# Seven-product weight pairs in a two-layer decoder trunk: a fourth pair, sums formed in place, and half of the plain low parts formed by accumulating DMA

## The chip, the cores and the metric

The kernel runs on one core of a Trainium2 chip. The metric is the device time of one execution in microseconds (us). The kernel before takes 2154.96 us, the median of three runs that lie between 2154.92 and 2155.69 us. A profile records one execution; its span runs from the first to the last instruction, and the execution's own time is a little longer.

## What is computed

Two pre-norm residual layers work on 256 tokens of width 2048. Each layer has a mixer (layer 0: sliding-window attention beside a matrix memory; layer 1: attention with forget gates) and then a SwiGLU block. The change touches only the SwiGLU block and what prepares its input:

```python
def swiglu(xn, w_gate, w_up, w_down):
    return (jax.nn.silu(xn @ w_gate) * (xn @ w_up)) @ w_down
# x: (256, 2048); w_gate, w_up: (2048, 5632); w_down: (5632, 2048); all float32
```

## The kernel before, in words

**Precision.** TensorE multiplies float32r tiles, which keep fewer bits than float32. So each operand is split into a high part (a cast, `hi`) and a low part (`lo`, the raw value minus the high part), and each block product is three matmuls: high times high, high times low, low times high (`three`, L350 to L353). The result is a 128x512 block in a PSUM bank.

**Chunks and half chunks.** The 16 blocks of the k axis (2048 / 128) are taken in eight pairs. `load_raw` (L94) brings two k blocks of 512 columns of one weight matrix, 512 KB, by one DMA of the SP queue into a raw tile of 128x1024. `split_chunk` (L147) makes `hi` on ACT (L150, a cast) and `lo` on DVE (L151, a subtraction). There are six `hi` and six `lo` tiles (pool `wp`) and four raw tiles (pool `wr`).

**The gate and up products.** The 5632 hidden columns are 11 groups of 512. For each group, `pair_group` (L358) works on both matrices and both token tiles of 128, over the eight k pairs, in the order of the tuple `ORDER`: each entry says whether the pair is plain (0) or mixed (1), and which k pair it is.

- A *plain* pair has 2 matrices x 2 k blocks x 2 token tiles = 8 block products, 24 matmuls. Its two half chunks (one of gate, one of up) are split as above.
- A *mixed* pair treats the same 2x2 blocks of x and of the weights by a scheme with 7 block products, 21 matmuls. Four weight sums are formed by DVE from the raw blocks (L386 to L389) into a tile `t4`, and `t4` is then split into `ht` (ACT, L246) and `lt` (DVE, L247) in two halves of 128x1024; the gate half chunk is split by L150 and L151, and one block of up by L246 and L247 with 128x512. The four sums of x blocks (`sx`) are made once per layer, when the mixer's output projection ends (`sums_of`, L208 to L216, called from `split_scaled`). Four of the seven products go to banks of their own (`prods`) and are combined once per group (L412 to L416).

Before the change three of the eight pairs are mixed: 5 x 24 + 3 x 21 = 183 matmuls for each group. Mixed pairs load into two raw tiles of the pool `fp`; `t4` has one buffer, `ht` and `lt` have two each.

**After the products.** DVE adds the two kinds of banks (L438), ACT takes the silu (L440), DVE multiplies (L442), TensorE transposes (L450, eight small matmuls per group), and the result is split into `mh` and `ml` (L246, L247).

**Down.** Hidden groups are taken in three parts per layer (3, 4 and 4 groups, `PARTS`). After each part the down projection over its 12 or 16 k blocks follows, with the same `pair_group` and one or two mixed pairs (`DOWN`). With 11 groups and two layers there are 22 gate and up groups in all.

**What sets the order.** The instructions of each engine run in program order, and that order is not the one of the source: the kernel is built with `schedule_with_timeline_sim=True`, so a planner simulates the program and places each instruction on its engine's queue by its own times. In the trace the matmuls of neighbouring pairs are therefore mixed with each other. Loads are issued from the SP queue, which holds nothing else; a load waits there until the tile it fills has been released. The POOL queue holds very little while the SwiGLU blocks run.

**Memory.** `dynamic_dma_scratch_size=8192` (L908) reserves that many bytes of every partition for the descriptors of DMAs that POOL issues.

Of the kernel before, what the change touches and what calls it, by code (L numbers as in the profile page):

```python
# [7 lines left out]
F32 = mybir.dt.float32  # L8
F32R = mybir.dt.float32r
AF = mybir.ActivationFunctionType  # L10
ALU = mybir.AluOpType
# [4 lines left out]
P = 128  # L16
D = 2048
# [4 lines left out]
NB = 512  # L22
CK = 2
# [7 lines left out]
OFF_QM, OFF_KM, OFF_VM, OFF_OM = 1536, 2048, 2560, 3584  # L31
CAP = 15.0
FILL = 24
ORDER = ((0, 0), (0, 1), (1, 2), (0, 4), (1, 3), (0, 5), (1, 6), (0, 7))
DOWN = {
    6: ((0, 0), (0, 1), (1, 2), (0, 3), (0, 4), (0, 5)),
    8: ((0, 0), (0, 1), (1, 2), (0, 3), (0, 4), (1, 5), (0, 6), (0, 7)),
# [11 lines left out]
def trunk(  # L49
# [20 lines left out]
    nc = tc.nc  # L70
# [7 lines left out]
    wr = ctx.enter_context(tc.tile_pool(name="wr", bufs=4))  # L78
# [15 lines left out]
    def load_raw(w, k0, c0, n, pool=wr):  # L94
        raw = pool.tile([P, CK, NB], F32, tag="raw", name="raw")
        nc.sync.dma_start(
            raw[:, :, 0:n], w[k0 * P : (k0 + CK) * P, c0 : c0 + n].rearrange("(k p) n -> p k n", p=P)
        )
        return raw
# [5 lines left out]
    for n in range(4):  # L105
# [7 lines left out]
        out=ident, in_=ident, pattern=[[-1, P]], compare_op=ALU.not_equal, fill=1.0, base=0, channel_multiplier=1  # L113
# [5 lines left out]
        out=upper, in_=ones, pattern=[[1, P]], compare_op=ALU.is_ge, fill=0.0, base=0, channel_multiplier=-1  # L119
# [20 lines left out]
    gain_columns(0)  # L140


    def load_chunk(w, k0, c0, n):
        raw = ahead.pop(0) if ahead else load_raw(w, k0, c0, n)
        return split_chunk(raw, n)

    def split_chunk(raw, n):  # L147
        hi = wp.tile([P, CK, NB], F32R, tag="hi", name="hi")
        lo = wp.tile([P, CK, NB], F32R, tag="lo", name="lo")
        nc.scalar.copy(hi[:, :, 0:n], raw[:, :, 0:n])  # L150
        nc.vector.tensor_tensor(  # L151
            out=lo[:, :, 0:n], in0=raw[:, :, 0:n], in1=hi[:, :, 0:n].bitcast(F32), op=ALU.subtract
        )
        return hi, lo
# [34 lines left out]
    sums = {}  # L189
# [55 lines left out]
    def split_plain(dst_h, dst_l, src):  # L245
        nc.scalar.copy(dst_h, src)  # L246
        nc.vector.tensor_tensor(out=dst_l, in0=src, in1=dst_h.bitcast(F32), op=ALU.subtract)  # L247
# [110 lines left out]
    def pair_group(fp, par, lhs, sums, mats, order):  # L358
        plain = [[bank(par, "acc") for _ in range(NT)] for _ in range(2)]
        prods = None  # L360
        kinds = [kind for kind, _ in order]
        t0, t1 = slice(0, P), slice(P, 2 * P)
        for pos, (kind, pair) in enumerate(order):
            k0 = 2 * pair
            if not kind:
                last = pos == len(order) - 1
                walk = [(i, t) for i in range(CK) for t in range(NT)]
                if last:
                    walk.sort(key=lambda it: it[1])
                for m, (w, c0) in enumerate(mats):  # L370
                    hi, lo = load_chunk(w, k0, c0, NB)
                    for i, t in walk:
                        ah, al = lhs(k0 + i)
                        ts = slice(t * P, (t + 1) * P)
                        three(
                            plain[m][t], ah[:, ts], al[:, ts], hi[:, i, :], lo[:, i, :],
                            pos == 0 and i == 0, last and i == CK - 1,
                        )
                continue
            first, last = 1 not in kinds[:pos], 1 not in kinds[pos + 1 :]  # L380
            if first:
                prods = [bank(1 - par, "prod") for _ in range(4)]
            ra, rb = (load_raw(w, k0, c0, NB, fp) for w, c0 in mats)
            hg, lg = split_chunk(ra, NB)
            t4 = fp.tile([P, 4, NB], F32, tag="t4", name="t4", bufs=1)
            nc.vector.tensor_tensor(out=t4[:, 0, :], in0=rb[:, 0, :], in1=ra[:, 0, :], op=ALU.subtract)  # L386
            nc.vector.tensor_tensor(out=t4[:, 1, :], in0=rb[:, 1, :], in1=rb[:, 0, :], op=ALU.subtract)
            nc.vector.tensor_tensor(out=t4[:, 2, :], in0=rb[:, 1, :], in1=t4[:, 0, :], op=ALU.subtract)
            nc.vector.tensor_tensor(out=t4[:, 3, :], in0=ra[:, 1, :], in1=t4[:, 2, :], op=ALU.subtract)  # L389
            hu = wp.tile([P, CK, NB], F32R, tag="hi", name="hi")  # L390
            lu = wp.tile([P, CK, NB], F32R, tag="lo", name="lo")
            split_plain(hu[:, 1, :], lu[:, 1, :], rb[:, 1, :])
# [20 lines left out]
        nc.vector.tensor_tensor(out=u2, in0=prods[3], in1=c[:, 0, :], op=ALU.add)  # L413
        nc.vector.tensor_tensor(out=c[:, 1, :], in0=prods[2], in1=u2, op=ALU.add)
        nc.vector.tensor_tensor(out=c[:, 2, :], in0=prods[1], in1=u2, op=ALU.add)
        nc.vector.tensor_tensor(out=c[:, 3, :], in0=prods[1], in1=c[:, 1, :], op=ALU.add)  # L416
        return plain, c

    def ffn(layer, fp, sx, sd, key, idx_next=None, key_next=None, finish=None):
# [6 lines left out]
        for g0, g1 in zip(PARTS, PARTS[1:]):  # L426
            end = g1 == PARTS[-1]
            nk = 4 * (g1 - g0)
            order = DOWN[nk // 2]
            for g in range(g0, g1):  # L430
                par = (g1 - 1 - g) % 2
                plain, c = pair_group(
                    fp, par, x_of, sums_x, [(w_gate[layer], g * NB), (w_up[layer], g * NB)], ORDER
                )
                for m in range(2):
                    for t in range(NT):
# [8 lines left out]
                for half in range(2):  # L445
# [5 lines left out]
                    pair = 2 * (g - g0) + half  # L451
# [22 lines left out]
            gf = None  # L474
            wd = w_down[layer][4 * g0 * P : 4 * g1 * P, :]
            for n0 in (0, 2):
# [7 lines left out]
                    fp, 1 - n0 // 2, m_of, sums_d, [(wd, n0 * NB), (wd, (n0 + 1) * NB)], order  # L484
                )
                if end and idx_next is None:
                    gf = fp.tile([P, D], F32, tag="t4", name="gf", bufs=1)
                    nc.gpsimd.dma_start(gf, norm_final.partition_broadcast(P))
                for m in range(2):
                    for t in range(NT):  # L490
# [23 lines left out]
    with tc.tile_pool(name="ev", bufs=1) as ev:  # L514
# [138 lines left out]
        with tc.tile_pool(name="mp", bufs=1) as mp:  # L653
            dt_ = mp.tile([P, ML_H, NT, P], F32, name="dt_")
            for g in range(2):
                pb = pm.tile([P, 2, NT, P], F32, tag="pm", name="pb")
                for i in range(2):
# [7 lines left out]
                    op=ALU.add,  # L665
# [257 lines left out]
```

## Time and profile before

| What | Before |
|---|---|
| median of three runs | 2154.96 us |
| profiled execution, its own time | 2154.99 us |
| its span | 2153.3 us |
| TensorE matmul (PE) busy | 2137.1 us, 99% of the span |
| VectorE (DVE) busy | 1668.7 us, 77% |
| ScalarE (ACT) busy | 1164.1 us, 54% |
| GpSimd (POOL) busy | 37.7 us, 2% |
| DMA from the SP queue, share of the 16 DMA engines | 58.3% |
| granted TensorE clock, mean | 0.998 |

Busy time is the time in which an engine works on at least one instruction; neighbouring instructions overlap, so the distance from start to start is what one of them costs, not its own duration. A wait row says which engine waited, at which line, and for what. A window row gives the busy time of each engine inside one stretch of the span, and the share of the DMA engines. In group rows the shapes stand as partitions x elements.

### The profile page before, as it was taken

The page shows a single profiled execution, that of the slowest core. Times are in us where ns is not written, and L with a number is a line of the kernel's source. Part 1 is how long each engine was busy: PE and PEld are TensorE (multiplying, and loading weights), DVE is VectorE, ACT ScalarE, POOL GpSimd, SP SyncE. Part 2 cuts the span into 40 slices and gives each one's busy share as a digit, 9 for nine tenths or more (in the row PEclk, how much of TensorE's full clock was granted, in tenths as well). Part 3 has the DMA queues.
Part 4 walks back from the last instruction along what each step waited for, and adds up shares of the span by engine and source line. Part 5 has one row for each costly group of instructions (what it writes and reads, how often), then busy time and mean ns, then how long its engine had stood idle before and what let it go on. Part 6 is the DMA issues. An engine that isn't in the chain of part 4 may idle for free.

```text
span 2153.3 us, 27002 instructions
## 1 busy us (share of the span) xinstructions
PE 2137.1 (99%) x9932; PEld 1774.6 (82%) x9932; DVE 1668.7 (77%) x2136; ACT 1164.1 (54%) x1514; POOL 37.7 (2%) x61
## 2 busy tenths in 40 slices
PE   8999999999999999999999999999999999999998
PEld 7888888888888888888888888888888888888886
DVE  6665567898889988998755555668988898888984
ACT  6564455655555545655545444555655555555553
POOL 2010000000000000000010000000000000000000
PEclk9999999999999999999999999999999999999999
DMA  8444555656665666656575554656556566656563
GB/s 266 147 157 145 169 171 191 208 194 203 203 201 180 210 195 205 200 191 196 160 234 166 166 177 149 212 176 205 195 192 206 190 200 209 196 199 203 178 213 127
DMA packets 213541, 408.37 MB, mean 190 GB/s; under 512 B 12736, under 2 KB 21024, under 8 KB 213152
## 3 DMA queue, kind: packets, MB, share of 16 engines
q1 hardware_dynamic: 212736, 402.90, 58.3%
q0 software_dynamic: 624, 3.72, 0.5%
q8 instruction: 78, 1.28, 0.2%
q14 instruction: 55, 0.45, 0.1%
q10 hardware_dynamic: 48, 0.02, 0.0%
HBM read 404.48 MB, written 2.11 MB: 189 GB/s over the span
## 4 chain that ended last, share of the span: by engine, by line
PE 98%; ACT 1%; issue 0%; DMA 0%; DVE 0%; DVEq 0%; POOLq 0%; POOL 0%; ACTq 0%
PE acc L353 17%; PE acc L352 17%; PE acc L351 17%; PE acc L173 10%; PE acc L175 10%; PE acc L174 10%; PE prod L353 4%; PE prod L352 4%; PE prod L351 4%; PE pf L450 1%; PE pt L224 1%; PE p L275 1%; PE ptm L258 1%; PE po L326 1%; PE pp L318 0%
## 5 line engine op out<-in xcount | busy, mean ns | idle before, releaser
L150 ACT CAST hi<-raw 128x1024 fp32r<-128x1024 f32 (+1 forms) x692 | 707.5, 1033 | 648.5 <-PE acc L353 314.3
L151 DVE TENSOR_TENSOR lo<-raw,hi 128x1024 fp32r<-128x1024 f32 (+1 forms) x692 | 825.7, 1201 | 288.1 <-ACT hi L150 285.9
L352 PE MATMUL acc<-lo,xh 128*128 128x512 f32 x946 | 368.4, 389 | 0.0
L353 PE MATMUL acc<-hi,xl 128*128 128x512 f32 x946 | 367.5, 391 | 0.0
L351 PE MATMUL acc<-hi,xh 128*128 128x512 f32 x946 | 365.2, 389 | 0.0
L173 PE MATMUL acc<-hi,xh 128*128 128x512 f32 (+3 forms) x736 | 276.8, 377 | 0.7 <-ACT hi L150 0.7
L175 PE MATMUL acc<-hi,xl 128*128 128x512 f32 (+3 forms) x736 | 276.9, 377 | 0.0
L174 PE MATMUL acc<-lo,xh 128*128 128x512 f32 (+3 forms) x736 | 276.4, 375 | 0.0
L247 DVE TENSOR_TENSOR lt<-t,ht 128x1024 fp32r<-128x1024 f32 x168 | 200.1, 1219 | 28.8 <-ACT ht L246 27.8
L246 ACT CAST ht<-t 128x1024 fp32r<-128x1024 f32 x168 | 174.6, 1053 | 81.1 <-PE prod L353 44.3
L352 PEld LDWEIGHTS acc<-lo,xh 128*128 128x128 f32 x946 | 177.6, 188 | 37.0
L353 PEld LDWEIGHTS acc<-hi,xl 128*128 128x128 f32 x946 | 177.6, 188 | 36.3
L351 PEld LDWEIGHTS acc<-hi,xh 128*128 128x128 f32 x946 | 177.7, 188 | 36.1
L352 PE MATMUL acc<-lo,mh 128*128 128x512 f32 x514 | 200.4, 390 | 0.0
L353 PE MATMUL acc<-hi,ml 128*128 128x512 f32 x514 | 199.4, 389 | 0.0
L351 PE MATMUL acc<-hi,mh 128*128 128x512 f32 x514 | 198.9, 389 | 0.0
L173 PEld LDWEIGHTS acc<-hi,xh 128*128 128x128 f32 x736 | 139.0, 189 | 24.9 <-ACT hi L150 1.1
L175 PEld LDWEIGHTS acc<-hi,xl 128*128 128x128 f32 x736 | 139.1, 189 | 24.4 <-issue 0.8
L174 PEld LDWEIGHTS acc<-lo,xh 128*128 128x128 f32 x736 | 139.1, 189 | 24.0 <-issue 0.7
L173 PE MATMUL acc<-hi,mh 128*128 128x512 f32 x320 | 125.8, 393 | 1.2 <-ACT mh L246 1.2
L174 PE MATMUL acc<-lo,mh 128*128 128x512 f32 x320 | 125.7, 393 | 0.0
L175 PE MATMUL acc<-hi,ml 128*128 128x512 f32 x320 | 124.0, 390 | 0.0
(299 smaller groups left out, 2726.8 us busy)
## 6 DMA issues: line engine op xcount, KB each, us to landing
raw<-in_w_gate_dram SPq DMA_DIRECT2D x176, 512.0 KB, 3.8
raw<-in_w_up_dram SPq DMA_DIRECT2D x176, 512.0 KB, 4.4
raw<-in_w_down_dram SPq DMA_DIRECT2D x176, 512.0 KB, 4.3
raw<-in_w_in_odd_dram SPq DMA_DIRECT2D x88, 512.0 KB, 3.8
raw<-in_w_in_even_dram SPq DMA_DIRECT2D x64, 512.0 KB, 4.2
raw<-in_w_out_even_dram SPq DMA_DIRECT2D x32, 512.0 KB, 3.7
raw<-in_w_out_odd_dram SPq DMA_DIRECT2D x32, 512.0 KB, 4.0
raw<-in_w_in_odd_dram SPq DMA_DIRECT2D x8, 272.0 KB, 2.8
```

The costliest lines, as they stand in the source:

```text
L150: nc.scalar.copy(hi[:, :, 0:n], raw[:, :, 0:n])
L151: nc.vector.tensor_tensor(out=lo[:, :, 0:n], in0=raw[:, :, 0:n], in1=hi[:, :, 0:n].bitcast(F32), op=ALU.subtract)
L173: nc.tensor.matmul(o, ah[:, ts], hi, start=(k == 0), stop=False)
L174: nc.tensor.matmul(o, ah[:, ts], lo, start=False, stop=False)
L175: nc.tensor.matmul(o, al[:, ts], hi, start=False, stop=(k == k_all - 1))
L224: nc.tensor.transpose(pt[:, i, t, :], h[:, t, k * P : (k + 1) * P], ident)
L246: nc.scalar.copy(dst_h, src)
L247: nc.vector.tensor_tensor(out=dst_l, in0=src, in1=dst_h.bitcast(F32), op=ALU.subtract)
L258: nc.tensor.transpose(pt[:, i, :], s_, ident)
L351: nc.tensor.matmul(o, ah, hi, start=start, stop=False)
L352: nc.tensor.matmul(o, ah, lo, start=False, stop=False)
L353: nc.tensor.matmul(o, al, hi, start=False, stop=stop)
```

## The change

1. **A fourth mixed pair.** `ORDER` has the mixed pairs 2, 3, 5, 6 in place of 2, 3, 6, and their order changes: before, plain and mixed pairs alternate in the middle (0, 1, *2*, 4, *3*, 5, *6*, 7; mixed ones in italics); after, two mixed pairs follow each other twice (0, 1, *2*, *3*, 4, *5*, *6*, 7). A group has 4 x 24 + 4 x 21 = 180 matmuls. `sx` grows to four pairs, and `sums_of` runs once more in each layer.
2. **Sums in place.** A mixed pair loads both matrices into one tile `r4` of 128x2048 with two buffers. The four sums overwrite its blocks, after the parts that need the raw blocks have been made; `t4` is gone. The kinds and sizes of DVE and ACT instructions in a mixed pair stay the same.
3. **Low parts by DMA.** For the plain pairs 0, 1, 4 and 7 (`BY_DMA`, all that are left) the up half chunk's low part is no longer a DVE subtraction. ACT writes minus the high part into `lo` (a second pass over 128x1024), and then POOL issues two DMAs of 128x512 that add the raw values to it (`accum_op=ALU.add`), tile to tile.
4. **Descriptor memory.** `dynamic_dma_scratch_size` goes from 8192 to 4096.

```diff
-ORDER = ((0, 0), (0, 1), (1, 2), (0, 4), (1, 3), (0, 5), (1, 6), (0, 7))
+ORDER = ((0, 0), (0, 1), (1, 2), (1, 3), (0, 4), (1, 5), (1, 6), (0, 7))
+BY_DMA = (0, 1, 4, 7)
...
+    def split_chunk(raw, n, by_dma=False):
         hi = wp.tile([P, CK, NB], F32R, tag="hi", name="hi")
         lo = wp.tile([P, CK, NB], F32R, tag="lo", name="lo")
         nc.scalar.copy(hi[:, :, 0:n], raw[:, :, 0:n])
+        if by_dma:
+            nc.scalar.mul(lo, hi.bitcast(F32), -1.0)
+            for i in range(CK):
+                nc.gpsimd.dma_start(lo[:, i, :].bitcast(F32), raw[:, i, :], accum_op=ALU.add)
+            return hi, lo
...
-                    hi, lo = load_chunk(w, k0, c0, NB)
+                    hi, lo = load_chunk(w, k0, c0, NB, by_dma=m == 1 and pair in by_dma)
...
-            ra, rb = (load_raw(w, k0, c0, NB, fp) for w, c0 in mats)
-            hg, lg = split_chunk(ra, NB)
-            t4 = fp.tile([P, 4, NB], F32, tag="t4", name="t4", bufs=1)
-            nc.vector.tensor_tensor(out=t4[:, 0, :], in0=rb[:, 0, :], in1=ra[:, 0, :], op=ALU.subtract)
-            nc.vector.tensor_tensor(out=t4[:, 1, :], in0=rb[:, 1, :], in1=rb[:, 0, :], op=ALU.subtract)
-            nc.vector.tensor_tensor(out=t4[:, 2, :], in0=rb[:, 1, :], in1=t4[:, 0, :], op=ALU.subtract)
-            nc.vector.tensor_tensor(out=t4[:, 3, :], in0=ra[:, 1, :], in1=t4[:, 2, :], op=ALU.subtract)
+            r4 = fp.tile([P, 4, NB], F32, tag="r4", name="r4")
+            for m, (w, c0) in enumerate(mats):
+                load_raw(w, k0, c0, NB, r4[:, 2 * m : 2 * m + 2, :])
+            hg, lg = split_chunk(r4[:, 0:2, :], NB)
...
+            b11, b21, b12, b22 = (r4[:, i, :] for i in range(4))
+            split_plain(hu[:, 1, :], lu[:, 1, :], b22)
+            nc.vector.tensor_tensor(out=b22, in0=b22, in1=b12, op=ALU.subtract)
+            nc.vector.tensor_tensor(out=b12, in0=b12, in1=b11, op=ALU.subtract)
+            nc.vector.tensor_tensor(out=b11, in0=b22, in1=b11, op=ALU.add)
+            nc.vector.tensor_tensor(out=b21, in0=b21, in1=b11, op=ALU.subtract)
             ht, lt = [], []
-            for i in range(2):
+            for i in (1, 0):
                 hs = fp.tile([P, 2, NB], F32R, tag="ht", name="ht")
                 ls = fp.tile([P, 2, NB], F32R, tag="lt", name="lt")
-                split_plain(hs, ls, t4[:, 2 * i : 2 * i + 2, :])
+                split_plain(hs, ls, r4[:, 2 * i : 2 * i + 2, :])
...
-    nc = _bacc.Bacc("TRN2", target_bir_lowering=False, num_devices=1, dynamic_dma_scratch_size=8192)
+    nc = _bacc.Bacc("TRN2", target_bir_lowering=False, num_devices=1, dynamic_dma_scratch_size=4096)
```

More of the change, by code (lines that the diff above doesn't have):

```diff
@@ L92, in trunk, with load_raw @@
     nc.scalar.dma_start(gn[0], norm_mix.rearrange("l (k p) -> (l k) p", p=P))
-    def load_raw(w, k0, c0, n, pool=wr):
-        raw = pool.tile([P, CK, NB], F32, tag="raw", name="raw")
+    def load_raw(w, k0, c0, n, raw=None):
+        if raw is None:
+            raw = wr.tile([P, CK, NB], F32, tag="raw", name="raw")
         nc.sync.dma_start(
@@ L140, in trunk, with load_chunk @@
     gain_columns(0)
-    def load_chunk(w, k0, c0, n):
+    def load_chunk(w, k0, c0, n, by_dma=False):
         raw = ahead.pop(0) if ahead else load_raw(w, k0, c0, n)
-        return split_chunk(raw, n)
-    def split_chunk(raw, n):
+        return split_chunk(raw, n, by_dma)
+    def split_chunk(raw, n, by_dma=False):
         hi = wp.tile([P, CK, NB], F32R, tag="hi", name="hi")
@@ L356, in bank, with pair_group @@
         return pm.tile([P, NB], F32, tag="pm", name=name) if par else pa.tile([P, NB], F32, tag="acc", name=name)
-    def pair_group(fp, par, lhs, sums, mats, order):
+    def pair_group(fp, par, lhs, sums, mats, order, by_dma=()):
         plain = [[bank(par, "acc") for _ in range(NT)] for _ in range(2)]
@@ L432, in ffn @@
                 plain, c = pair_group(
-                    fp, par, x_of, sums_x, [(w_gate[layer], g * NB), (w_up[layer], g * NB)], ORDER
+                    fp, par, x_of, sums_x, [(w_gate[layer], g * NB), (w_up[layer], g * NB)], ORDER, BY_DMA
                 )
@@ L486, in ffn @@
                 if end and idx_next is None:
-                    gf = fp.tile([P, D], F32, tag="t4", name="gf", bufs=1)
+                    gf = fp.tile([P, D], F32, tag="r4", name="gf")
                     nc.gpsimd.dma_start(gf, norm_final.partition_broadcast(P))
```

1 line of the change is left out of this document (removed).

## The prediction

> **What bounds the kernel now.** I read four things in turn: busy shares, the chain of work that ended last, the waits of TensorE (PE), and PE's timeline inside one group of the SwiGLU block.
>
> ```profile
> span 2153.3 us, 27002 instructions
> PE 2137.1 (99%) x9932; PEld 1774.6 (82%) x9932; DVE 1668.7 (77%) x2136; ACT 1164.1 (54%) x1514; POOL 37.7 (2%) x61
> PE 98%; ACT 1%; issue 0%; DMA 0%; DVE 0%; DVEq 0%; POOLq 0%; POOL 0%; ACTq 0%
> ```
> ```profile
> PE pg L137 <- DMA gn<-in_norm_mix_dram: 4.0, 1, 4.0
> PE acc L173 <- ACT mh L246: 1.2, 1, 1.2
> ...
> PE pp L318 <- DVE s L310: 0.2, 1, 0.2
> ```
> ```profile
> 419.60 0.39 PE L351 MATMUL acc<-hi,xh 128*128 128x512 f32 x1
> ...
> 424.81 0.39 PE L353 MATMUL acc<-hi,xl 128*128 128x512 f32 x1
> ```
>
> PE is 98% of the chain. Its waits (five rows; the first two and the last are shown) all lie at lines of the mixer or the start; none names L351 to L353, the products of the SwiGLU blocks. The two timeline rows are the first and the last of 24 matmuls: 23 steps in 5.21 us, 0.2265 us each. A matmul taken away is therefore worth 0.2265 us, as long as nothing else comes late. How near the others are is in the windows: one period of a gate and up group (43 us) and a longer stretch.
>
> ```profile
> core 0: us, PE busy (x) PEld busy (x) DVE busy (x) ACT busy (x) POOL busy (x), PEclk, DMA share, GB/s
> 404.00:447.00 43.00, 43.00 (x196) 35.59 (x194) 38.61 (x47) 24.57 (x28) 0.00 (x0) 1.00 0.61 197
> 595.00:728.00 133.00, 133.00 (x600) 110.23 (x599) 121.81 (x152) 77.38 (x88) 0.00 (x0) 1.00 0.60 196
> ```
>
> PE has no gap, at full clock. DVE is at 90% to 92%, ACT at 57%, POOL at nothing, the DMA engines at 61%. So DVE is the second bound, and the change must not add to it.
>
> **The matmuls.** A pair that turns from plain to mixed has 21 matmuls in place of 24: 3 x 22 groups = 66, by 0.2265 us = **14.95 us** less on the path.
>
> **DVE per group.** Durations overlap, so the step from one start to the next counts.
>
> ```profile
> 428.53 0.69 DVE L389 TENSOR_TENSOR t<-raw,t 128x512 f32<-128x512 f32 x1
> 429.14 2.35 DVE L151 TENSOR_TENSOR lo<-raw,hi 128x1024 fp32r<-128x1024 f32 x2
> 431.41 0.69 DVE L413 TENSOR_TENSOR u<-prod,c 128x512 f32<-128x512 f32 x1
> 432.01 2.35 DVE L247 TENSOR_TENSOR lt<-t,ht 128x1024 fp32r<-128x1024 f32 x2
> 434.27 0.69 DVE L414 TENSOR_TENSOR c<-prod,u 128x512 f32<-128x512 f32 x1
> ```
>
> A 128x512 operation costs 0.61 us (428.53 to 429.14), a 128x1024 one 1.135 (two in 2.27). A plain pair is two of the large: 2.27. A mixed pair is three large and five small: 6.46. The fourth mixed pair adds 4.19 us; the four low parts that go to DMA take away 4 x 1.135 = 4.54. DVE falls by 0.35 to 38.3 us, in a period that falls from 43.1 to 42.4 (43.0 in the window is rounded; 3 x 0.2265 = 0.68 less): still 90%. Of the sums in place I take nothing: the same operations, only in a fixed order.
>
> **ACT per group.**
>
> ```profile
> L150 ACT CAST hi<-raw 128x1024 fp32r<-128x1024 f32 x660 | 687.5, 1053 | 614.7 <-PE acc L353 307.5 <-PE acc L175 230.4 <-issue 38.0
> L246 ACT CAST hi<-raw 128x512 fp32r<-128x512 f32 x84 | 52.3, 622 | 87.1 <-PE acc L353 68.0 <-issue 13.0 <-ACT ht L246 4.2
> L859 ACT ACTIVATE junk<-h 128x512 f32<-128x512 f32 x8 | 5.0, 627 | 13.5 <-DVE h L857 13.5
> ```
>
> The negated copy isn't in this trace; an ACTIVATE of 128x512 takes 627 ns where a cast takes 622, so I price it as the large cast, 1.05 us. Four of them are 4.2 us; the mixed pair adds 3 x 1.05 + 0.62 - 2 x 1.05 = 1.7. ACT goes from 24.6 to 30.5 of 42.4 us, 72%. It is covered by what ACT does most of the time now: L150 waits 307.5 us for PE to release a tile.
>
> **The accumulating DMAs: the unknown.** Each group gets 8, of 256 KB, on the POOL queue.
>
> ```profile
> q1 hardware_dynamic: 212736, 402.90, 58.3%
> q0 software_dynamic: 624, 3.72, 0.5%
> ...
> raw<-in_w_gate_dram SPq DMA_DIRECT2D x176, 512.0 KB, 3.8
> raw<-in_w_up_dram SPq DMA_DIRECT2D x176, 512.0 KB, 4.4
> ...
> raw<-in_w_in_even_dram SPq DMA_DIRECT2D x8, 256.0 KB, 3.1
> ...
> gf<-in_norm_final_dram POOLq DMA_DIRECT2D x1, 1024.0 KB, 5.0
> ```
> ```profile
> L488 POOL DMA_DIRECT2D gf<-in_norm_final_dram x1 | 0.6, 587 | 639.1 <-issue 639.1
> ```
>
> *Engine time.* A load packet (one row of 2 KB) costs 0.583 x 16 x 2153.3 / 212736 = 94 ns. Eight DMAs of 128 rows over 16 engines are 64 rows per engine and group. The lower bound of a row is a load row, 94 ns; the upper one is the mean packet of POOL's queue, 0.005 x 16 x 2153.3 / 624 = 276 ns, though those packets are larger (6 KB). An accumulate reads two rows and writes one, so I take two load rows, 189 ns, which also lies in the middle: 12.1 us per group beside the 0.61 x 43 = 26.2 us of loads, 38.3 of 42.4, 90%. The bounds give 76% and 103%. [...]
>
> *Delay.* An up chunk's low part now passes ACT twice (2 x 1.05), two POOL issues (2 x 0.59, from L488) and the transfer. There are six `hi` tiles, so a tile comes free five half chunks ahead of its use: 5 x 12 x 0.2265 = 13.6 us. That leaves 10.3 us for the transfer; the nearest rows are 3.1 us for 256 KB and 5.0 for 1 MB from POOL. I take it as hidden. Past 10.3 us, each of 88 chunks would cost PE what it is late.
>
> *What queues behind it.* The raw tile is released only when the accumulate has read it, and the next load waits for that on SP, with all later loads behind it.
>
> ```profile
> SPq L96 <- DVE lo L151: 1406.0, 578, 10.6
> ```
>
> SP already waits so most of the time. Four raw tiles serve 8 plain half chunks per 42.4 us, one use in 21 us; an up chunk holds its tile for 4.4 + 2.1 + 1.2 + about 5 = 12.7 us, a gate chunk 3.8 + 2.2 = 6. There is room.
>
> **Two mixed pairs in a row.** `ht` and `lt` have two tiles each, one pair's worth. The second pair's cast waits until PE has used the first pair's. A case of that chain, and its use:
>
> ```profile
> 419.84 1.05 ACT L246 CAST ht<-t 128x1024 fp32r<-128x1024 f32 x1 [0.31 <-PE acc L353]
> ```
> ```profile
> 420.51 2.36 DVE L247 TENSOR_TENSOR lt<-t,ht 128x1024 fp32r<-128x1024 f32 x2
> ```
> ```profile
> 427.08 0.39 PE L351 MATMUL prod<-ht,sx 128*128 128x512 f32 x1
> ```
>
> From PE's release to the last `lt` are 3.0 us (419.84 to 422.87), and PE uses them 4.2 us later, for a plain pair's 5.4 us lie between. In source order nothing would lie between: from the first pair's last product to the second pair's last two sums are 15 matmuls, 3.4 us, so 0.4 us of reserve. The planner can put plain matmuls in between, as it does now. I take no stall; a stall costs 1 us per us late, at 44 places.
>
> **Once per layer.** `sums_of` runs for one more pair.
>
> ```profile
> 358.72 0.69 DVE L386 TENSOR_TENSOR t<-raw 128x512 f32<-128x512 f32 x1 [3.12 <-DMA raw<-in_w_up_dram]
> ...
> 366.31 0.28 DVE L215 TENSOR_TENSOR s<-full,s 128x128 f32<-128x128 f32 x1
> ```
>
> Four operations of 0.28 us and a split of 0.69 are 1.8 us of DVE; just there DVE stands idle for 3.12 us, which hides it. Without that cover it would be 2 x 1.8 = 3.6 us at most. The descriptor memory costs nothing: POOL's queue holds eight DMAs in 42 us. The layer's mixer and the down products keep their work.
>
> **Sum.** The profiled execution took 2154.99 us by its own time (span 2153.3; the median of the runs is 2154.96, the same within 0.03). 2154.99 - 14.95 = **2140.0 us**, 0.7% faster. Its own range is 2137 to 2146: up to 0.3 us of new waits per group.
>
> **Rivals.**
>
> *A. The DMA engines become the bound (slower).* The point from which it decides is (42.4 - 26.2) / 64 = 253 ns per accumulated row; the period of before is reached at (43.1 - 26.2) / 64 = 264 ns. At the upper bound of 276 ns the period is 26.2 + 17.7 = 43.9 us, 1.5 more than forecast, 22 x 1.5 = 33: 2173 us. For it: nothing in this trace accumulates, and a read, a read and a write one after another would be 3 x 94 = 283 ns. Against it: the loads themselves, also a read and a write, take only 94. Chance 0.18.
>
> *B. The doubled mixed pairs stall PE.* For it: 0.4 us of reserve where 4.2 are now, on in-order queues, and DVE at 90%. Against it: the planner's freedom. It uses up the gain at 14.95 / 44 = 0.34 us per place. At 0.3 us it gives 2153 us, at 0.6 us 2166. Chance 0.20: 0.08 within 0.2%, 0.10 slower, 0.02 still faster.
>
> *C. POOL's issues hold up DVE.* If the two could not work at the same time, DVE would have 38.3 + 8 x 0.59 = 43.0 of 42.4 us: +0.6 per group, 2153 us. [...] Chance 0.06.
>
> *D. The change doesn't do what it says:* the accumulated low parts land past their 10.3 us, so that PE waits for the very parts that were to be out of its way. At 0.3 us late per chunk, 88 x 0.3 = 26: 2166 us. Chance 0.03.
>
> **How the numbers follow.** The forecast has 0.53. Faster by over 0.2% (below 2150.7; about what a measurement here can tell from no change): 0.53 + 0.02 = 0.55. Within 0.2%: 0.08 + 0.06 = 0.14. Slower: 0.18 + 0.10 + 0.03 = 0.31. The range 2137 to 2175 takes in the forecast, C, nearly all of B, the upper bound of the row price and D; what is left out is an accumulate dearer than 276 ns or a delay of many us, about 0.14, and 0.03 below.
>
> **What would show it.** Right: no wait of PE at L351 to L353, 66 products fewer, DVE near 38 us per period, the DMA share in gate and up windows near 0.9, the period 42.4. Wrong by A: that share near 1.0, and DVE or ACT waiting for raw tiles. Wrong by B: PE waiting for L247 `lt`. By D: PE waiting for DMA into `lo`. By C: 1.135 us steps of DVE stretched wherever POOL issues. What I may have missed is an order of the planner that suits its own times for the accumulates but not the chip's.

## The result, and the profile after

The changed kernel takes 2309.9 us (median of 4 runs, 2304.21 to 2316.29); before takes 2154.94 beside it. The ratio is 1.0719 (95% interval 1.0684 to 1.0755): 155 us slower, where 15 us faster was forecast. Line numbers of after are 2 higher than before's near L150, 7 near L350 and some 9 near L400.

The page of after, with the lines that answer to those of before:

```profile
span 2303.6 us, 27356 instructions
...
PE 2186.8 (95%) x9866; PEld 1768.2 (77%) x9866; DVE 1671.8 (73%) x2190; ACT 1271.5 (55%) x1652; POOL 190.8 (8%) x237
...
q1 hardware_dynamic: 212736, 402.90, 53.3%
q0 software_dynamic: 25968, 49.87, 11.9%
...
PE 70%; DMA 13%; ACT 7%; DVE 7%; issue 3%; SPq 0%; POOL 0%; ACTq 0%; DVEq 0%; POOLq 0%
...
lo<-raw POOLq DMA_DIRECT2D x176, 256.0 KB, 7.1
```

The 66 matmuls are gone (9932 to 9866), yet PE is busy 50 us longer and is only 70% of the chain, not 98%. VectorE's total has hardly moved (1668.7 to 1671.8), as forecast. The waits of PE (total, times, longest) are no longer those of the mixer:

```profile
PE acc L359 <- DMA lo<-raw: 63.7, 28, 4.7
PE prod L358 <- ACT hi L152: 15.0, 13, 1.9
PE acc L358 <- ACT hi L152: 11.9, 10, 2.2
PE prod L358 <- ACT ht L253: 5.4, 14, 0.5
```

These make 96 of the 170 us between 2310 and the forecast. A part of the rest is clock. Here are three stretches of after in the windows view, the first of them one whole group, then the clock over the whole span (after, and the later run without transfers, whose label is e10_neg_only):

```profile
core 0: us, PE busy (x) PEld busy (x) DVE busy (x) ACT busy (x) POOL busy (x), PEclk, DMA share, GB/s
616.00:666.00 50.00, 44.19 (x187) 34.23 (x186) 36.66 (x47) 28.17 (x33) 6.96 (x8) 0.97 0.76 219
```
```profile
645.90:649.40 3.50, 0.00 (x0) 0.00 (x0) 2.54 (x3) 2.98 (x4) 0.96 (x2) 1.00 1.04 269
649.50:652.80 3.30, 2.89 (x7) 2.34 (x8) 0.05 (x1) 0.00 (x0) 1.76 (x2) 0.50 1.11 261
```
```profile
core 0: 2303.6 us, clock 0.984
```
```profile
core 0: 2214.7 us, clock 0.996
```

A group takes about 50 us where 42.4 were forecast. After a wait of 4.1 us (645.8 to 649.9) PE runs 3.3 us at a clock of 0.50, which costs another 1.7 us of work; over the span up to 0.016 x 2303.6 = 37 us are lost to the clock, by its mean. In this trace a stretch at 0.50 follows each of the seven waits of over 4 us inside the SwiGLU blocks and eight waits of 1.5 to 3.1 us; other waits of up to 2.7 us have none behind them. The DMA share of the group is 0.76, but 1.04 in the wait and 1.11 behind it: transfers come in a bunch. The chain of work that ended last, in that group (start, length, what):

```profile
625.90 4.56 DMA r<-in_w_gate_dram
630.49 1.05 ACT hi L152
631.59 0.50 PE prod L358
...
640.70 0.94 ACT ht L253
641.64 0.48 ACT c L421
642.12 0.97 ACT lo L154
643.10 0.28 issue
643.38 6.48 DMA lo<-raw
649.91 0.80 PE acc L359
```

Two links in turn hold PE. The first is the load of a mixed pair (625.90). The `lt` that frees its own tile was done at 622.9; the load stood on SyncE's queue behind the load of an up chunk, which waited for its raw tile until an accumulate had landed (SyncE's waits from 617 to 631 us):

```profile
SPq L98 <- DMA lo<-raw: 8.5, 1, 8.5
```

The three other mixed loads of this group (630.54, 643.69 and 649.58) were issued within 0.03 us of the `lt` that frees their tile. The second link is an accumulate whose negation stood behind other work of ScalarE (642.12) and which then took 6.5 us to land. Which of these is the cause, and which only the place where it shows, is what the experiments had to tell.

### The profile page after: what moved, and what is told of

The parts are those of the page before. It is cut to its first block, busy times and chain, and to the rows that moved or that the text cites. A ratio compares the mean times of both kernels' runs of the same rounds, so it can differ in the third digit from the quotient of the medians.

```text
span 2303.6 us, 27356 instructions
## 1 busy us (share of the span) xinstructions
PE 2186.8 (95%) x9866; PEld 1768.2 (77%) x9866; DVE 1671.8 (73%) x2190; ACT 1271.5 (55%) x1652; POOL 190.8 (8%) x237
## 3 DMA queue, kind: packets, MB, share of 16 engines
q0 software_dynamic: 25968, 49.87, 11.9%
## 4 chain that ended last, share of the span: by engine, by line
PE 70%; DMA 13%; ACT 7%; DVE 7%; issue 3%; SPq 0%; POOL 0%; ACTq 0%; DVEq 0%; POOLq 0%
PE acc L359 10%; PE acc L360 10%; PE acc L358 10%; PE acc L180 10%; PE acc L181 10%; PE acc L182 10%; DMA lo<-raw 6%; ACT hi L152 3%; DMA r<-in_w_up_dram 3%; DMA r<-in_w_gate_dram 3%; PE prod L359 2%; PE prod L360 2%; PE prod L358 1%; DVE lt L254 1%; ACT ht L253 1%
## 5 line engine op out<-in xcount | busy, mean ns | idle before, releaser
L152 ACT CAST hi<-raw 128x1024 fp32r<-128x1024 f32 (+3 forms) x564 | 571.3, 1027 | 533.0 <-PE acc L182 263.9
L158 DVE TENSOR_TENSOR lo<-raw,hi 128x1024 fp32r<-128x1024 f32 (+3 forms) x476 | 562.7, 1188 | 273.3 <-ACT hi L152 271.6
L359 PE MATMUL acc<-lo,xh 128*128 128x512 f32 x792 | 320.2, 404 | 63.7 <-DMA lo<-raw 63.7
L254 DVE TENSOR_TENSOR lt<-r,ht 128x1024 fp32r<-128x1024 f32 x212 | 257.1, 1218 | 62.4 <-ACT ht L253 62.2
L156 POOL DMA_DIRECT2D lo<-raw x176 | 152.9, 1120 | 1599.8 <-ACT lo L154 1580.9
L253 ACT CAST ht<-r 128x1024 fp32r<-128x1024 f32 x212 | 221.5, 1047 | 71.4 <-PE prod L360 44.9
L152 ACT CAST hi<-r 128x1024 fp32r<-128x1024 f32 x106 | 111.4, 1051 | 241.1 <-PE acc L360 147.1
L358 PE MATMUL acc<-hi,mh 128*128 128x512 f32 x514 | 198.9, 391 | 6.9 <-ACT hi L152 6.9
L359 PE MATMUL acc<-lo,mh 128*128 128x512 f32 x514 | 200.8, 391 | 0.0
L360 PE MATMUL acc<-hi,ml 128*128 128x512 f32 x514 | 198.8, 389 | 0.0
L158 DVE TENSOR_TENSOR lo<-r,hi 128x1024 fp32r<-128x1024 f32 x106 | 129.3, 1220 | 72.0 <-ACT hi L152 71.7
```

What stands on the lines that cost most here:

```text
L156: nc.gpsimd.dma_start(lo[:, i, :].bitcast(F32), raw[:, i, :], accum_op=ALU.add)
L158: nc.vector.tensor_tensor(out=lo[:, :, 0:n], in0=raw[:, :, 0:n], in1=hi[:, :, 0:n].bitcast(F32), op=ALU.subtract)
L358: nc.tensor.matmul(o, ah, hi, start=start, stop=False)
L359: nc.tensor.matmul(o, ah, lo, start=False, stop=False)
L360: nc.tensor.matmul(o, al, hi, start=False, stop=stop)
```

## The experiments

The theories by name: **L**, the accumulated low parts land too late; **A**, the DMA engines are the bound; **H**, two `ht` and two `lt` tiles stall the second of two mixed pairs; **R**, two `r4` tiles: the loads of a mixed pair wait until the pair two before it is split. "Now" is the changed kernel at 2310.

### Each part alone

**e2_in_place**: the old order, sums in place, no transfers.

```diff
-ORDER = ((0, 0), (0, 1), (1, 2), (1, 3), (0, 4), (1, 5), (1, 6), (0, 7))
-BY_DMA = (0, 1, 4, 7)
+ORDER = ((0, 0), (0, 1), (1, 2), (0, 4), (1, 3), (0, 5), (1, 6), (0, 7))
+BY_DMA = ()
```


> The kernel before with one part of the change alone: sums in place in r4 and the smaller descriptor memory; the old order with three mixed pairs, no low part by DMA. Theory L: the same work in another buffer, 2150 to 2160 us. Theory B: r4 alone already delays its loads, 2170 us or more.

Measured 2155.09, ratio 1.0002 (0.9992 to 1.0012). With three mixed pairs apart the sums in place cost nothing.

**e3_dma_alone**: the old order, `BY_DMA = (0, 1, 4, 7)` kept.

> The old order with three mixed pairs that stand apart, sums in place, and the up low parts of four of the five plain pairs (0, 1, 4, 7) by DMA; pair 5 stays with DVE. DVE has 4.5 us per group less to do than before. Theory L: PE waits for lo as in the changed kernel, 2230 us or more. Theory B: with the mixed pairs apart the waits are gone, 2150 to 2175 us.

Measured 2156.48, ratio 1.0007 (0.9998 to 1.0017). One group of it in the windows view, and its page's row of the accumulates:

```profile
616.00:658.40 42.40, 42.40 (x192) 35.15 (x191) 35.43 (x47) 28.93 (x34) 6.94 (x8) 1.00 0.89 248
```
```profile
lo<-raw POOLq DMA_DIRECT2D x176, 256.0 KB, 6.2
```

The DMA engines run at 0.89 and PE has no gap: A is refuted, and the price per row with it confirmed. An accumulate lands after 6.2 us, and nobody waits.

**e1_no_dma**: the new order with `BY_DMA = ()`, the low parts back on VectorE.

> The changed kernel with BY_DMA empty: four mixed pairs in the new order, sums in place, and every low part by a DVE subtraction again. Theory L (the accumulated low parts land later than the order of PE allows, and all else follows from that): the 64 us in which PE waits for lo, its half clock after the long waits and the late r loads vanish; DVE gets 4 x 1.135 = 4.5 us per group back, 42.9 of a 42.4 us period, so 2150 to 2170 us. Theory B (the two mixed pairs in a row and the in-place tile r4 hold PE up, and the DMAs only add to it): the waits for ACT at L152 (31 us of PE) and the late r loads stay, 2220 us or more.

Measured 2270.19, ratio 1.0537 (1.0522 to 1.0553). With four mixed pairs the loss comes without any transfer; but VectorE has 42.9 us of work here in a group of 42, so this run alone doesn't say why.

**e7_double3**: three mixed pairs, two of them in a row, no transfers.

```diff
+ORDER = ((0, 0), (0, 1), (1, 2), (1, 3), (0, 4), (0, 5), (1, 6), (0, 7))
+BY_DMA = ()
```


> The kernel e2_in_place (three mixed pairs, no DMA low parts, 2155 us) with pairs 2 and 3 put next to each other: 0, 1, 2, 3, 4, 5, 6, 7 with 2, 3, 6 mixed. One double in each group, DVE as in the kernel before. Theory H: half the doubles of e1_no_dma, so about half its loss of 115 us: 2200 us or more. Theory R: the shortest way from a mixed pair to the next but one is two mixed and two plain pairs, 20 us: 2150 to 2165 us.

Measured 2154.26, ratio 0.9998 (0.9988 to 1.0007). With three mixed pairs H costs nothing; with four, see e16_floor.

### The fourth pair with the transfers: first attempts

**e4_copy**: the transfers copy instead of adding (`accum_op` dropped; the order of the instructions on every engine stays).

> The changed kernel with the 176 accumulating DMAs turned into plain copies of the same tiles and sizes on the same queue, in the same order on every engine. It leaves out the addition: the low parts are wrong, so only the time counts. It separates the price of the addition in the DMA engine (184 ns per row) from the path to it (two ACT passes, POOL's issue, landing). If the price of the row is what makes the parts late (rival A of the prediction): a row takes about 95 ns, the parts land 3 us sooner where several are queued, and half or more of the loss of 155 us goes: 2230 us or less. If it is the path and the place in the order (theory L): landing stays above 4.5 us and the time above 2250 us.

Measured 2273.56 (one run, no interval). The landing falls to 5.7 us and 36 us go; most of the loss stays, so the addition isn't the main part.

**e5_even**: the mixed pairs two by two, with two plain pairs between.

```diff
+ORDER = ((0, 0), (1, 2), (1, 3), (0, 1), (0, 4), (1, 5), (1, 6), (0, 7))
```


> The changed kernel with its four mixed pairs still in two doubles, but two plain pairs between the doubles on both sides: 0, 2, 3, 1, 4, 5, 6, 7 with 2, 3, 5, 6 mixed. Theory R (the two r4 tiles: a mixed pair can load only when the low parts of the pair two before it are made, and load, split, sums and split again take about 20 us, while the changed order leaves two mixed and one plain pair, 15 us, between them): every tile now has two mixed and two plain pairs, 20 us, so most of the loss goes: 2145 to 2190 us. Theory H (ht and lt have two tiles each, one pair's worth, so doubled pairs stall whatever lies between the doubles): as many doubles as before, 2250 us or more.

Measured 2335.55, ratio 1.0846 (1.0821 to 1.0871): slower than now. This spoke against R.

**e8_r4_three** and **e9_ht_three**: three `r4` tiles, or three `ht` and three `lt` tiles, each paid for with a chunk tile (`wp` 6 to 5).

```diff
-    wp = ctx.enter_context(tc.tile_pool(name="wp", bufs=6))
+    wp = ctx.enter_context(tc.tile_pool(name="wp", bufs=5))
-            r4 = fp.tile([P, 4, NB], F32, tag="r4", name="r4")
+            r4 = fp.tile([P, 4, NB], F32, tag="r4", name="r4", bufs=3)
```


> The changed kernel with three r4 tiles; room for it comes from the hi and lo tiles, five in place of six, which takes 2.7 us from the lead of the plain chunks. Theory R: the load of a mixed pair no longer waits for the pair two before, at least half of the loss goes, 2230 us or less. Theory H: no change or worse, 2290 us or more.

> The changed kernel with three ht and three lt tiles, and five hi and lo tiles as in e8_r4_three. Theory H: the second pair of a double can be split half a pair earlier, 2230 us or less. Theory R: the lateness comes from the load, 2290 us or more.

Measured 2294.67, ratio 1.0644 (1.0628 to 1.066), and 2295.09, ratio 1.065 (1.0634 to 1.0666): 15 us each. In e8_r4_three PE waits even more for the accumulates than now:

```profile
PE acc L359 <- DMA lo<-raw: 74.6, 39, 5.7
```

So neither R nor H seemed to hold. The mistake lay in the design: with the accumulates late anyway, relief elsewhere can't show, and the sixth chunk tile was taken from the accumulates' own lead.

### Without the accumulates

**e10_neg_only**: the two transfers left out, the rest of the changed kernel kept; low part = negated high part.

```diff
             nc.scalar.mul(lo, hi.bitcast(F32), -1.0)
-            for i in range(CK):
-                nc.gpsimd.dma_start(lo[:, i, :].bitcast(F32), raw[:, i, :], accum_op=ALU.add)
```


> The changed kernel with the four accumulating transfers per group left out: the low part of the four up chunks is then only the negated high part, so this run leaves out the addition, and 66 matmuls fewer, four mixed pairs, the sums in place and ScalarE's negations stay. VectorE has 38.3 us of work per group as in the changed kernel and no matmul waits for a transfer between tiles. Late accumulates only (what costs is that matmuls wait for a transfer that lands 6 to 7 us after its issue): about 2140, as first predicted. Load on VectorE (the loss of the variant without transfers, 2270, came from 42.9 us of VectorE work in a group of 42.4 us): also about 2140. The tiles r4 and the order of the four pairs (a mixed pair's loads wait until the pair two before it is split): a good part of the loss stays, 2200 or more.

Measured 2215.7, ratio 1.028 (1.0263 to 1.0297). 94 us of the loss are the accumulates', 61 above before are not. The chain in one group shows what those are:

```profile
656.83 1.06 ACT ht L253
657.91 1.22 DVE lt L254
659.13 0.48 DVE sd L254
659.65 1.23 DVE lt L254
660.89 3.67 DMA r<-in_w_gate_dram
664.63 0.91 issue
665.54 1.05 ACT ht L253
666.63 0.73 PE prod L358 x2
```

PE has used the first pair's `ht` (656.5); only then is the second pair's `ht` cast, then its `lt`; only then is its `r4` tile free and the next pair's load issued (660.9); and PE waits for what follows from that load: ScalarE's cast of it, at 664.6, stands ahead of the `ht` cast for which PE waits. This is R, with H as its first link.

**e12_neg_r4three**: the same with three `r4` tiles and five chunk tiles.

> The run without the transfers (the low part of the four up chunks is the negated high part, the addition is left out), with three r4 tiles and five chunk tiles instead of two and six. If the two r4 tiles set the time, it falls to within 15 us of 2140 while the run with two stays above 2200. If the accumulates or VectorE's load set it, both are near 2140. If both stay above 2200, it is neither: the order of the four pairs or the lead of the chunk tiles.

Measured 2167.92, ratio 1.0062 (1.0047 to 1.0077): 48 us less than with two. Its largest wait of PE is now

```profile
PE prod L358 <- ACT ht L253: 9.0, 22, 0.5
```

**e13_neg_even**: e5_even's order without the accumulates.

> The run without the transfers (addition left out), with the pairs in the order plain, mixed, mixed, plain, plain, mixed, mixed, plain. With the transfers this order gave 2335, more than the changed order's 2310. If the transfers made the difference there (plain chunks closer together), it is here no slower than the run without transfers in the changed order; if the run of two mixed pairs itself costs, it is alike too; if the r4 tiles' turn (two mixed pairs, then a pause of two plain ones) sets the time, it is some 10 to 40 us faster.

Measured 2181.64, ratio 1.0127 (1.0112 to 1.0142): 34 us less than e10_neg_only, within the 10 to 40 that R gives, since two plain pairs then lie between one doubled pair and the next in every place. Half of the 34 us is one wait, in e10_neg_only and then in this run:

```profile
PE acc L358 <- ACT hi L152: 18.9, 7, 3.6
```
```profile
PE acc L358 <- ACT hi L152: 1.8, 2, 1.0
```

In e10_neg_only it lies where a down projection begins, whose first mixed pair needs an `r4` tile too (at 719.8 us its load is issued right behind the `lt` that frees one). R holds; e5_even had hidden it behind late accumulates.

**e11_free_low**: e10_neg_only without the negations too (`lo = hi`).

> As the run without the transfers, and ScalarE's negations are left out too: the matmuls of the four up chunks take the high part in the place of the low part (this leaves out the low part). ScalarE falls by some 4 us per group. If ScalarE's negations, standing in line before later casts, cost something, it is faster than the run with them; else the two are alike within 5 us. Tiles r4 and the order of the pairs: 2200 or more here too. VectorE's load or late accumulates: about 2140.

Measured 2227.33, ratio 1.0339 (1.0324 to 1.0355). ScalarE's 4 us are not the cause. That it is 12 us slower was expected by no theory; the instructions stand in another order on every engine, and I leave it open.

**The turn of an r4 tile**, worked out from the traces: from the issue of a gate load to the issue of the load that follows in the same tile, mean over the turns that lie whole within two stretches of consecutive groups (us; n turns).

```
                 n  load  to cast  to sums  sums  to last lt  to issue  turn
e3_dma_alone     5  4.94   8.63     5.73    4.07    3.64       0.78    27.79   three pairs
e7_double3       5  3.82   7.85     6.49    6.32    4.52       0.03    29.03   three pairs
e10_neg_only    16  4.87   0.12     5.76    6.50    5.22       0.03    22.49
e1_no_dma       16  4.30   0.17     6.99    7.73    5.36       0.03    24.59
e18_not_seven   16  5.23   0.12     6.67    7.25    5.83       0.31    25.40
after           16  6.50   2.12     5.68    5.23    5.89       0.19    25.61
e12_neg_r4three  7  3.93   8.87     7.22    6.67    5.20       0.03    31.91   three tiles
e8_r4_three     12  5.82   9.75     5.96    6.77    5.82       0.41    34.52   three tiles
```

"To cast" is the slack: the tile lies loaded and waits for ScalarE. With three pairs it is 8 us, with two tiles and four pairs little or nothing, with three tiles 9 us again. Four pairs in two tiles leave each turn (42.40 - 0.68) / 2 = 20.9 us (42.40 is the group of e3_dma_alone, less three matmuls). It takes 22.5 without transfers (2 x 22.5 = 45.0 a group), 24.6 when VectorE has more (49.2), 25.6 in the changed kernel (51.2). The mean hides two kinds of turn. In e10_neg_only the turns inside a group, from pair 2 to 5 and from 3 to 6, take 18.3 to 19.0 us without any slack, while PE's work between them, two mixed pairs and a plain one, is 66 x 0.2265 = 15.0 us; those across to the next group take 26.0 to 26.5.

### Why the accumulates cost 94 us on top

**e14_double3_dma**: e7_double3 with `BY_DMA = (0, 1, 4, 7)`.

> Three mixed pairs, two of them in a row (positions three and four of the eight), and the four accumulating transfers per group; r4 two tiles, six chunk tiles as in the changed kernel. Without the transfers this order gave 2154. If two mixed pairs in a row hold ScalarE up so long that the accumulates behind them come too late, 2180 or more. If the fourth pair is needed (VectorE at 38 of 42 us, the r4 tiles' turn), within 5 us of 2155.

Measured 2184.92, ratio 1.0157 (1.0132 to 1.0181). **e17_dma_five**: e3_dma_alone with five chunk tiles.

> The old order with three mixed pairs apart and the four accumulating transfers, with five chunk tiles instead of six, which takes 2.7 us off the lead that a transfer has. With six it gave 2156. If lead is what the accumulates lack, 2170 or more, with matmuls that wait for the transfers; if three pairs leave enough, within 3 us of 2156.

Measured 2177.31, ratio 1.0105 (1.009 to 1.012). The waits of PE for accumulates, in e14_double3_dma and in e17_dma_five:

```profile
PE acc L359 <- DMA lo<-raw: 16.9, 22, 1.6
```
```profile
PE acc L359 <- DMA lo<-raw: 11.2, 17, 1.4
```

With three mixed pairs apart and six chunk tiles the accumulates just fit. Two mixed pairs in a row, free without them (e7_double3), cost 31 us with them; one chunk tile less costs 21 (not run without them). So the lead has no reserve, and L holds in this sense.

**e15_dve_less**: the changed kernel with the plain gate chunks' low parts left out.

```diff
+        if by_dma is None:
+            return hi, hi
-                    hi, lo = load_chunk(w, k0, c0, NB, by_dma=m == 1 and pair in by_dma)
+                    hi, lo = load_chunk(w, k0, c0, NB, by_dma=None if m == 0 and by_dma else m == 1 and pair in by_dma)
```


> The changed kernel with the low parts of the four plain gate chunks left out (the matmuls take the high part in their place): VectorE has 4.5 us less per group, 33.8 of some 42, as much spare time as with three pairs; transfers, order and tiles as in the changed kernel. If VectorE's lost spare time makes the accumulates late, 2140 to 2180. If it is the lead of the chunk tiles or the r4 tiles' turn, 2270 or more. In between: both have a share.

Measured 2269.53, ratio 1.0549 (1.0518 to 1.058). VectorE's load is worth 40 us, the smaller part. **e16_floor**: the same cut on e12_neg_r4three.

> Four mixed pairs with everything relieved: no transfers between tiles (the addition is left out), the gate chunks' low parts left out, three r4 tiles and five chunk tiles. If only waits ate the gain, the 66 matmuls fewer show here: 2140 to 2146. If it stays at the 2168 of the run with VectorE's full load, the rest of 28 us comes from the doubled pairs (ht and lt), not from VectorE.

Measured 2156.41, ratio 1.0008 (0.9998 to 1.0017): neither 2140 to 2146 nor 2168. Even with all of this relieved the fourth pair gains nothing over before; of the 16 us above 2140 the trace names 6.8 as waits of PE for `ht` (12 times, 0.7 at most). That is not all, for a wait row counts only time in which PE does nothing: a matmul's record lasts 0.39 us, a step 0.2265, and a matmul that starts up to 0.16 us late leaves no gap. One of the 12 places:

```profile
647.31 1.05 ACT L255 CAST ht<-r 128x1024 fp32r<-128x1024 f32 x1 [4.00 <-PE prod L362]
```
```profile
648.41 0.73 PE L360 MATMUL prod<-ht,sx 128*128 128x512 f32 x2
649.87 0.50 PE L360 MATMUL prod<-ht,sx 128*128 128x512 f32 x1 [0.73 <-ACT ht L255]
```

ScalarE stands for 4.00 us until PE has used the first pair's `ht`; then it casts the second pair's, and PE is late at each piece. This is H. Added up over the traces, what the steps between matmuls of 128x512 last beyond 0.2265 us is 29.1 us here and 14.2 in before (steps that are over 0.02 us too long). Of the 14.9 more, 13.5 lie at products with `ht`, where before has none. So the 66 matmuls fewer do give their 15 us here, and the doubled pairs take them back. In e12_neg_r4three the sum is 40.8, of which products with `ht` and `lt` have 27.5: nearly all of the 28 us by which that run misses 2140.

**e18_not_seven**: `BY_DMA = (0, 1, 4)`.

> The changed kernel with three accumulating transfers per group instead of four: the up chunk of the last plain pair gets its low part on VectorE again (39.4 us of VectorE work per group instead of 38.3). In the changed kernel's trace the matmul waits for an accumulate fall nearly all on that chunk, 64 us of 69, and the halved clock behind them. If that one chunk is the accumulates' price, it falls to about the 2216 of the run without transfers plus a few us for VectorE, 2215 to 2240. If another chunk is late next, or if the accumulates load every stage alike, it keeps more than two thirds of the 94 us: 2280 or more.

Measured 2304.24, ratio 1.0701 (1.0677 to 1.0724). A miss, and the most telling one. Its waits of PE:

```profile
PE acc L358 <- ACT hi L152: 44.3, 20, 3.6
PE prod L358 <- ACT hi L152: 16.9, 16, 2.1
PE prod L358 <- ACT ht L253: 14.3, 26, 1.9
PE prod L359 <- DVE lt L254: 8.4, 16, 0.5
PE acc L359 <- DMA lo<-raw: 7.1, 13, 1.5
```

The wait for accumulates is gone (63.7 to 7.1), the time is not: the waits have moved to the casts. In the table its turn is as long as in after: a faster load and no wait for the cast (3.3 us less), but 3 us more at VectorE. I read the accumulate as the last link of a full turn, not as the reason why the turn was full. VectorE's 1.1 us more per group are some 10 of the 88 us that stay, by the 40 us that 4.5 us are worth in e15_dve_less (an estimate).

**e19_raw_free**: the accumulates read a part of `xh`, so that the raw tile is free after its cast. SyncE's load queue, after and then this run:

```profile
SPq L98 <- DVE lo L158: 1089.6, 403, 10.6
SPq L98 <- DMA lo<-raw: 401.1, 86, 9.0
SPq L98 <- DVE lt L254: 236.9, 78, 8.8
```
```profile
SPq L98 <- DVE lo L158: 1150.0, 400, 20.1
SPq L98 <- DVE lt L254: 404.8, 85, 12.4
```


> The changed kernel with accumulating transfers of the same number and size that read a part of xh, which nothing writes in that time, instead of the raw tile (the low parts of the four up chunks come out as other values, which leaves the right addition out). The raw tile is free again after its cast, the matmuls still wait for each transfer, the traffic is the same. If the raw tile held until the landing (12 to 14 us after the cast's start), with the loads of the mixed pairs queued behind it on SyncE, is the accumulates' price, it falls by 50 us or more, to 2260 or less. If it is the landing itself or the traffic beside the loads, it stays within 20 us of 2310.

Measured 2314.7, ratio 1.0737 (1.0719 to 1.0755). The queue's 401 us wait for landings goes, the wait for `lt` grows by 168, and the time stays. The held raw tile is not the price.

## Why the prediction was wrong, point by point

**Two mixed pairs in a row: the step that failed.** The prediction took no stall there and put the sums in place at nothing ("the same operations, only in a fixed order"). It counted the `ht` and `lt` tiles and not the two `r4` tiles, in which the sums are now formed, so that they are held until the last `lt`. Their turn runs through `ht` and `lt`: a doubled pair holds its `r4` tile longer, and the next pair's load starts that much later. A group has two turns per tile, 20.9 us each; without accumulates they take 22.5. The 170 us between the forecast and 2310 come off in three steps, in the order in which the runs relieve them:

- 94 us with the accumulates (e10_neg_only, 2215.7);
- 48 us more with a third `r4` tile (e12_neg_r4three, 2167.9);
- the last 28 us are, by the steps of PE in e12_neg_r4three, the stall at `ht` and `lt` itself.

In another order the shares differ: the third tile gave 15 us while the accumulates were there (e8_r4_three). The last part is rival B: its price of 0.6 us at 44 places gave 2166 us, about what e12_neg_r4three took, and 0.3 us gave 2153, near e16_floor's 2156. It looked for the waits at `lt`, where the traces have them mostly at `ht`, and it missed the `r4` tiles behind them. With three mixed pairs the doubled pair costs nothing (e7_double3).

**Delay: mis-sized.** "About 5 us" for the transfer was 7.1 at the median, and from the start of the cast to the last landing the four chunks of a group take 14.0, 12.5, 7.9 and 14.2 us on average (worked out from after's trace), against a lead of 13.6. That fits only while nothing upstream slips (e3_dma_alone); e14_double3_dma and e17_dma_five show how thin it is. In the full turns of after, against those of e10_neg_only, the loads take longer too (4.9 to 6.5 us), and so does the wait for the cast (0.1 to 2.1). From the transposes of one group to those of the next, the 16 steps that have no down projection between them sum to 826 us in after and to 746 in e10_neg_only: 80 of the 89 us between these two executions. By the mean clock, 28 us (0.016 x 2303.6 - 0.004 x 2214.7) of the 89 are halved clock. "There is room" for the raw tiles failed too, SyncE's queue waited 401 us for landings, but without that hold the time was the same (e19_raw_free). Rival D was this mechanism, at 0.3 us a chunk and 0.03 of the chance.

**What held.** 66 matmuls fewer. VectorE's sum (1671.8 us on the page). The accumulate's price: 0.119 x 16 x 2303.6 / 25968 = 169 ns a packet over that queue, and 184 ns for a 2 KB row of the accumulates alone (mean of their packet records), against 189 forecast and 99 for a 2 KB row of the loads by the same count. The price of two load rows was an estimate; 184 to 99 is 1.9 load rows, but no run shows that a second read is the reason. With plain copies in their place POOL's queue moved the same bytes in 5.6% of the 16 engines' span (e4_copy), with accumulates in 11.9% (after). Rival A fell with e3_dma_alone, at a share of 0.89. Rival C fell with after's trace: a step of 128x1024 on VectorE lasts 1.138 us where POOL issues (62 steps) and 1.139 elsewhere (460). The sums in place cost nothing by themselves (e2_in_place, three pairs).

**The sum.** 14.95 us for the matmuls were taken as certain once nothing was late. No run showed them in its time, and 2156.4 is the best that four pairs gave; in e16_floor's steps they are there, and the stall at `ht` is nearly as large.

**The warning** about an order that suits the planner's times was right in part: the negation at 642.12 stands behind casts that are less urgent. How much that costs by itself wasn't tried, and the runs don't separate it. The planner orders each kernel anew: of the runs without accumulates or with other ones, only e4_copy keeps after's order on PE, ScalarE and VectorE. In e10_neg_only 7985 of the 9866 matmuls stand at the same place of the order as in after, in e12_neg_r4three 6328 at the same place as in e10_neg_only (compared by their tiles' names). So the 94 and the 48 us hold a share of order, of unknown size.

**Still open**: which part of the accumulates' 94 us is the landing, which the traffic, which the queues and which the order (a plain copy took 36 us off, e4_copy; e18_not_seven and e19_raw_free, which take one link away each, next to nothing); why e11_free_low is slower than e10_neg_only; and how much of the 94 us a sixth chunk tile beside three `r4` tiles would take back (no run had both). No run had the four mixed pairs one by one between plain ones, and none had four pairs with a separate tile for the sums, so what the doubling costs apart from the fourth pair, and what the sums in place cost with four, is not shown.

## What to carry to other kernels

Before a tile changes its role, follow its whole turn, from load to the operation that frees it and to the next load, and hold it against the time that the new order leaves for it: engine shares of 90% and less said nothing about that here. A wait that a trace names most often may only be the last link of a full turn; take the link away and see whether the time goes or the wait moves. Add up the steps from start to start as well as the waits, for PE was late here without a gap: its records of 0.39 us overlap at steps of 0.2265. And when two limits are both near, relieve them together: relieved alone, each looked innocent here.

## What the runs showed of the hardware

In the changed kernel the nine waits of PE of over 3 us inside the SwiGLU blocks were all followed by a stretch at a clock of 0.50, of 3.4 or 6.8 us, and so were six waits of 1.5 to 2.8 us; others of up to 2.7 us were not (worked out from the clock records of after's trace). 3.4 us at 0.50 are 1.7 us of work. An accumulating transfer of 256 KB between tiles took 6.2 us at the median to land beside steady loads (e3_dma_alone) and 7.1 in the changed order (after), where POOL issued up to four within 3.5 us; plain copies in that order took 5.7 (e4_copy). The DMA engines ran at 0.89 over a whole group of 42.4 us in which PE had no gap (e3_dma_alone).
